# A two-layer diffusion trunk on one core: the tile scheduler ranks instructions by a simulated timeline

## The chip, the core and the metric

The kernel runs on one core of a Trainium2 chip. The core has five engines, each with a queue of its own that it works through in order: TensorE (PE in the profile; its weight loads are shown apart, as PEld), VectorE (DVE), ScalarE (ACT), GpSimd (POOL) and SyncE (SP, which here only issues DMA transfers). An instruction that needs another engine's result waits for a semaphore, and all that stands behind it in its queue waits with it. So the order in each queue is a part of the program, although it changes nothing in what is computed.

The metric is the device time of one execution in microseconds; below 1% matters here. The median of three runs of the kernel before is 1856.94 us.

## What is computed

Two layers over 512 latent tokens and 256 context tokens, width 1024. The first mixes by neighbourhood attention and spatial gating, the second by retention in both directions; each layer ends in a gated MLP with a convolution over three tokens. Everything is float32.

```python
for i in range(DEPTH):
    ...
    h_lat = modulate(rmsnorm(x, norm_g[i, 0]), sh1, sc1)
    h_ctx = modulate(rmsnorm(xc, norm_g[i, 0]), csh1, csc1)
    if i % 2 == 0:
        y_ctx, y_lat = hybrid_na_sgu(...)
    else:
        y_ctx, y_lat = retention_mixer(...)
    x = x + g1 * rmsnorm(y_lat, norm_g[i, 1])
    h = modulate(rmsnorm(x, norm_g[i, 2]), sh2, sc2)
    x = x + g2 * rmsnorm(conv_ffn(h, ...), norm_g[i, 3])
    ...

def conv_ffn(h, w_in, conv_w, conv_b, w_out):
    a = dwconv3(h @ w_in, conv_w, conv_b)
    gate, up = jnp.split(a, 2, axis=-1)
    return (jax.nn.silu(gate) * up) @ w_out
```

## The kernel before

Every float32 operand of a matmul is split into a high part, rounded by ACT, and a low part, the rest, subtracted by DVE (`split`, line 110); three matmuls (`mm3`, line 152) make a product of them: high by high, high by low, low by high. So each weight that a DMA brings in costs one ACT and one DVE instruction of about 1 us before PE can use it, and in the names of the profile `g` or `fo` stand for both parts. Most instructions are issued by one wrapper and so carry its line, L71; the names of the tiles tell them apart.

The stages, with their place in the profiled span:

- Start and spatial gating (0 to about 150 us): `sgu` (line 725) loads the tokens, makes the modulation rows `ad` from the ada weights (`ar`), and turns and scales the tokens (`xT`, `first_xT` line 1778) into the operands `h0a`/`h1a` (`first_h`, line 1788). The first products are `ug`, with weights `ug10` to `ug13` in four steps `q`; in the program each step makes its weights' split, then the three token chunks of h0a, then the products, with ada rows between.
- Attention (to about 400 us): head pairs; `take_qk` (line 946) makes the operands of the scores. `kb`, the low part of k beside itself, is made by DVE in pieces and then doubled by POOL (line 970). `pq`, `s`: projections and scores. The gate rows of later stages are made beside it (`acc <- ar` on DVE, 256 instructions in the whole kernel).
- First MLP, `ffn(0)` (line 1439; to about 930 us): 768 tokens, 22 blocks `j` of 128 hidden columns. Per block the two halves, gate and up, come from seven block products instead of eight: the accumulators `px`, `py`, `pz` take products with the weights `wa`, `wb` (from `s`), `wc` (from `q`) and `wd`; ACT and DVE move them to `pre` (`take`, `meet`), and `conv` (line 1531) makes `cv`, then `g`. The weights of block j+1 are prepared between the products of block j. The output product `wf` with weights `fo` is made per pair of blocks in 12 pieces that are strewn between products of later blocks; ACT copies each piece (`yp`, `ypg`) and POOL issues a DMA that adds it in memory. The last four blocks, 18 to 21, are left to `out_last` (line 635), which adds blocks 18 and 19 (group A, tiles `wf0A`) for the first tokens and then blocks 20 and 21 (group B) into the same accumulators.
- Retention (to about 1450 us): operands `h0c`/`h1c` from `build_h` (line 417), weights `rwv`, `rwg`, `wx` and others, products `rn`.
- Second MLP, `ffn(1)` (to the end): the same with 512 tokens; its last output groups (`wf1A`, `wf1C`) end the kernel.

What sets the order. The program is written as one sequence. [...] Which tiles share a buffer follows from the program, and so do all dependencies. Some stretches are exempt: between `hold(True)` and `hold(False)` (line 367) every instruction of DVE, ACT and PE is marked to keep its place in program order against other marked ones (`Ordered`, line 59). These marks stand around the closing output pieces (`out_pieces`, line 599, only where `final` is given), the norms behind them (`flush`, line 709) and the first products of an MLP. The products and convolutions of the blocks and the group A pieces of `out_last` are not marked:

```python
LAST = NF - 2 * GF
...
    product(X, d[22], hb(("t", 4)), "onto")
    take(pre, 1, 0, X)
    step()
    o(3)
    gs[j] = conv(j, pre)
...
self.out_group(*A, y, e, False, None, f"{name}A", "CB", held=held)
...
self.out_group(*B, y, e, False, final, f"{name}B", held=held)
```

## Time and profile before

| | before |
|---|---|
| median of 3 runs | 1856.94 us (1853.55 to 1860.03) |
| profiled execution | 1852.3 us, of this span 1850.5 us |
| PE, PEld, DVE, ACT, POOL busy | 96%, 86%, 75%, 56%, 18% |
| mean granted PE clock | 0.99 |
| DMA | 253.45 MB, mean 137 GB/s |

How to read it: a row of the timeline gives the start and the length of an instruction or of a run of equal ones, the engine, the line, the operation, out <- in by the program's names, the shape and the count; in brackets, how long the engine had been idle before it and what ended that. Rows of equal matmuls are drawn together, also where some stand among others. A row of the windows gives the busy time of each engine in a stretch, with the count, then the clock that PE was granted (1.00 is full speed), the busy share of the DMA engines and what they moved. The list of waits sums an engine's idle time by the operand that ended it.

### The profile page before, as it was taken

How to read it: one execution, taken by the hardware profiler on the slowest of the kernel's cores; microseconds unless marked ns; L12 is line 12 of the kernel's file. 1: busy time of each engine (PE TensorE's matmuls, PEld its weight loads, DVE VectorE, ACT ScalarE, POOL GpSimd, SP SyncE). 2: the span in 40 equal slices, each digit the busy share in tenths (PEclk: the TensorE clock that was granted, in tenths of full speed). 3: DMA queues.
4: the chain of work that ended last, by engine and by line, in shares of the span. 5: the costliest groups of instructions: out<-in, count | busy, mean ns of one | idle time of the engine just before them, and what ended most of it. 6: DMA issues, size and time to landing. Idle time of an engine off the chain costs nothing. (4 is left out here: it accounts for less than half of the span.)

```text
span 1850.5 us, 28777 instructions
## 1 busy us (share of the span) xinstructions
PE 1781.8 (96%) x10928; PEld 1582.7 (86%) x10928; DVE 1391.1 (75%) x2347; ACT 1029.3 (56%) x1866; POOL 330.0 (18%) x462
## 2 busy tenths in 40 slices
PE   7999899999999999999999999999999889999997
PEld 4888777679998899998888988988999789989996
DVE  4877675789878788787866676676656699988886
ACT  6533455677555565564664534344434467766763
POOL 1102122131122322222112011011101100222221
PEclk9999999999999999999999999999999989999999
DMA  7344321155577777786722422331321225877762
GB/s 297 112 141 143 117 82 36 55 171 148 178 156 168 174 175 161 156 173 151 265 97 92 143 99 80 125 113 58 105 69 60 101 82 157 215 197 201 171 161 97
DMA packets 84399, 253.45 MB, mean 137 GB/s; under 512 B 11026, under 2 KB 11538, under 8 KB 84260
## 3 DMA queue, kind: packets, MB, share of 16 engines
q1 hardware_dynamic: 55044, 191.27, 30.9%
q0 software_dynamic: 26912, 51.95, 16.4%
q10 hardware_dynamic: 2304, 8.39, 1.1%
q8 instruction: 86, 1.41, 0.3%
q14 instruction: 53, 0.43, 0.1%
HBM read 191.80 MB, written 39.85 MB: 125 GB/s over the span
## 5 line engine op out<-in xcount | busy, mean ns | idle before, releaser
L71 DVE SCALAR_TENSOR_TENSOR acc<-ar,cs,acc 128x512 f32<-128x512 f32 x256 | 185.7, 751 | 33.7 <-DMA ar<-in_adaw 24.7
L71 DVE SCALAR_TENSOR_TENSOR cv<-pre,cw,cv 128x769 f32<-128x769 f32 (+1 forms) x176 | 153.6, 884 | 4.9 <-ACT cv L71 4.2
L71 PE MATMUL rn<-rwv,h0c 128*128 128x256 f32 x768 | 136.3, 281 | 3.0 <-ACT h0c L71 3.0
L71 PEld LDWEIGHTS rn<-rwv,h0c 128*128 128x128 f32 x768 | 118.2, 191 | 3.7 <-ACT h0c L71 3.4
L71 PE MATMUL wf<-fo,g 128*128 128x512 f32 x432 | 112.6, 394 | 0.5 <-DVE fo L71 0.5
L71 PE MATMUL rn<-rwv,h1c 128*128 128x256 f32 x384 | 108.1, 282 | 0.4 <-DVE h1c L71 0.2
L1688 POOL DMA_DIRECT2D yf<-yp x64 | 55.1, 861 | 257.0 <-ACT yp L71 233.8
L71 ACT ACTIVATE cv<-pre,cw 128x770 f32<-128x770 f32 (+1 forms) x88 | 81.3, 925 | 24.0 <-DVE pre L71 23.4
L71 PE MATMUL rn<-rwg,h0c 128*128 128x256 f32 x512 | 90.0, 280 | 0.0
L71 PEld LDWEIGHTS wf<-fo,g 128*128 128x128 f32 x432 | 75.9, 188 | 13.8 <-DVE fo L71 1.4
L71 PE MATMUL px<-hs,wc 128*128 128x384 f32 (+1 forms) x480 | 79.3, 314 | 5.4 <-ACT pre L71 3.2
L71 PEld LDWEIGHTS px<-hs,wc 128*128 128x128 f32 x480 | 74.3, 191 | 10.8 <-ACT pre L71 5.4
L71 ACT ACTIVATE pre<-px 128x256 f32<-128x256 f32 (+2 forms) x160 | 54.3, 367 | 47.7 <-PE px L71 47.6
L71 ACT COPY yp<-wf 128x512 f32<-128x512 f32 x118 | 67.8, 576 | 19.0 <-PE wf L71 16.5
L71 PEld LDWEIGHTS rn<-rwg,h0c 128*128 128x128 f32 x512 | 78.1, 189 | 0.0
L71 PE MATMUL pz<-hb,wa 128*128 128x384 f32 (+1 forms) x480 | 77.3, 308 | 0.0
L71 PE MATMUL px<-hb,wa 128*128 128x384 f32 (+1 forms) x480 | 77.1, 308 | 0.0
L71 PE MATMUL py<-blk,wb 128*128 128x384 f32 (+1 forms) x480 | 76.9, 308 | 0.0
L71 PE MATMUL px<-blk,wb 128*128 128x384 f32 (+1 forms) x480 | 76.7, 309 | 0.0
L71 PEld LDWEIGHTS px<-hb,wa 128*128 128x128 f32 x480 | 73.2, 188 | 3.2
L71 PEld LDWEIGHTS px<-blk,wb 128*128 128x128 f32 x480 | 73.4, 189 | 3.0 <-ACT pre L71 0.2
L71 PEld LDWEIGHTS rn<-rwv,h1c 128*128 128x128 f32 x384 | 72.9, 190 | 1.5 <-DVE h1c L71 1.3
(1272 smaller groups left out, 5112.6 us busy)
## 6 DMA issues: line engine op xcount, KB each, us to landing
ar<-in_adaw SPq DMA_DIRECT2D x96, 512.0 KB, 3.9
yf<-yp POOLq DMA_DIRECT2D x64, 256.0 KB, 4.2
yd<-yp POOLq DMA_DIRECT2D x54, 256.0 KB, 5.0
yd<-ypg POOLq DMA_DIRECT2D x54, 256.0 KB, 4.9
fin<-xd SPq DMA_DIRECT2D x8, 512.0 KB
xn<-in_x SPq DMA_DIRECT2D x6, 512.0 KB, 4.6
xb<-in_x SPq DMA_DIRECT2D x6, 512.0 KB
xd<-xb ACTq DMA_DIRECT2D x6, 512.0 KB, 2.8
```

Source lines behind the costliest of these rows:

```text
L71: i = f(*args, **kw)
L1688: G.dma_start((yd[t] if first else y[t])[:, o], v, accum_op=ALU.add)
```

## The change

One argument at the place where the framework is opened:

```diff
-    with tile.TileContext(nc) as tc, ExitStack() as ctx:
+    with tile.TileContext(nc, schedule_with_timeline_sim=True) as tc, ExitStack() as ctx:
         Trunk(ctx, tc, a, out).build()
```

[...] The order within each engine's queue changes, and with it which instruction carries a wait.

## The prediction

> **What bounds the kernel now.** I read the summary of the page first, then the chain of waits, the waits of PE, and the windows; times within the span count from its start.
>
> ```profile
> span 1850.5 us, 28777 instructions
> ...
> PE 1781.8 (96%) x10928; PEld 1582.7 (86%) x10928; DVE 1391.1 (75%) x2347; ACT 1029.3 (56%) x1866; POOL 330.0 (18%) x462
> ...
> PE 35%; DVE 7%; DMA 3%; ACT 2%; issue 1%; POOL 1%; ACTq 0%; DVEq 0%; POOLq 0%
> ```
>
> TensorE is busy for 1781.8 of 1850.5 us, and both kernels issue the same matmuls. So an order can gain at most what PE stands idle, 1850.5 - 1781.8 = 68.7 us, and it can lose without such a limit. The waits of PE say where these idle times lie (columns: total, times, longest).
>
> ```profile
> PE ht L71 <- DVE xn L71: 9.4, 1, 9.4
> PE s L71 <- POOL kb L970: 7.1, 1, 7.1
> PE pf L71 <- ACT hb L71: 5.9, 1, 5.9
> PE px L71 <- ACT pre L71: 3.2, 4, 1.2
> ...
> PE at L71 <- ACT arow L71: 2.4, 1, 2.4
> PE px L71 <- ACT wc L71: 2.2, 1, 2.2
> PE wf L71 <- ACT ypg L71: 2.1, 2, 1.6
> ...
> PE wf L71 <- DVE fo09l L71: 1.8, 1, 1.8
> ```
>
> No wait is large. The first (9.4, the first load) and `pf <- hb` (5.9, the norm between retention and the second MLP) stand at places whose order the two kernels share; they stay. The windows add the engines behind PE and the clock:
>
> ```profile
> core 0: us, PE busy (x) PEld busy (x) DVE busy (x) ACT busy (x) POOL busy (x), PEclk, DMA share, GB/s
> 435.00:445.00 10.00, 9.18 (x51) 8.43 (x50) 10.00 (x13) 10.00 (x16) 0.00 (x0) 1.00 0.17 52
> ...
> 500.00:850.00 350.00, 346.60 (x1802) 320.62 (x1801) 281.23 (x401) 201.52 (x348) 92.08 (x117) 1.00 0.76 167
> ...
> 1550.00:1851.00 301.00, 288.81 (x1972) 265.12 (x1971) 256.10 (x398) 192.58 (x346) 62.73 (x76) 0.99 0.67 172
> ...
> 190.00:197.00 7.00, 4.93 (x13) 4.06 (x14) 6.03 (x10) 5.43 (x11) 3.88 (x2) 0.51 0.47 149
> 640.00:644.00 4.00, 4.00 (x13) 3.37 (x13) 4.00 (x8) 2.69 (x4) 1.17 (x2) 0.58 0.75 180
> 862.00:870.00 8.00, 8.00 (x44) 7.49 (x43) 6.18 (x11) 3.61 (x7) 2.61 (x3) 1.00 0.84 228
> ```
>
> Inside the MLPs PE is full (346.6 of 350), with DVE behind it at 80% (281.23) and 85% (256.10); at the head of the first MLP DVE and ACT have no free time at all. The last three rows are for the clock, below.
>
> **The change, part by part.** It adds and removes no instruction: comparing the two programs, every name and operation has its partner. 6195 of 10832 matmuls, 1448 of 2251 DVE, 1012 of 1730 ACT, 71 of 462 POOL and 86 of 400 SP instructions stand in another place of their queue. A matmul that is moved among others costs nothing by itself, since the matmuls run back to back (40 in 9.31 us, below); what costs is an operand that is now late for its place. So I laid the new order over the times of the profiled run and looked for places where an instruction would come before its operand. Nearly all that I found are at stage borders.
>
> Second MLP, last product (+4.4):
>
> ```profile
> 1817.47 1.65 PE L71 MATMUL px<-hs 128*128 128x256 f32 x12
> 1818.95 9.31 PE L71 MATMUL wf1A<-fo,g 128*128 128x512 f32 x40
> ...
> 1819.15 0.38 ACT L71 ACTIVATE pre<-px 128x256 f32<-128x256 f32 x1 [0.23 <-PE px L71]
> ...
> 1822.79 0.63 ACT L71 ACTIVATE g<-cv 128x512 fp32r<-128x512 f32 x1 [1.63 <-DVE cv L71]
> ...
> 1823.46 0.69 DVE L71 TENSOR_TENSOR g<-cv,g 128x512 fp32r<-128x512 f32 x1 [0.70 <-ACT g L71]
> ```
>
> The last product px ends at 1819.1; evacuation, convolution and gate take until the high part g is there (1822.79 + 0.63 = 1823.4) and its low part (1824.15). Now 24 output matmuls of earlier blocks, 24 x 9.31 / 40 = 5.6 us, lie over this chain. The new order puts 21 of the 24 ahead of the last product and leaves 3. The work is the same, but the chain starts 21 x 0.233 = 4.9 us later and PE has 0.7 us to do instead of 5.6: by the times, PE would stand 4.4 us ahead of the high part, 4.7 of the low. I take 4.4; if the chain ran faster with DVE and ACT less loaded, 3.5.
>
> First MLP, last product (+6.5), the same mechanism with longer tiles:
>
> ```profile
> 894.38 2.25 PE L71 MATMUL px<-hs,wd 128*128 128x384 f32 x12
> ...
> 897.40 0.40 PE L71 MATMUL wf0A<-fo018h,g 128*128 128x512 f32 x1
> ...
> 903.54 0.40 PE L71 MATMUL wf0A<-fo020h,g 128*128 128x512 f32 x1
> ...
> 901.97 0.85 ACT L71 ACTIVATE g<-cv 128x770 fp32r<-128x770 f32 x1 [2.21 <-DVE cv L71]
> ...
> 902.85 0.96 DVE L71 TENSOR_TENSOR g<-cv,g 128x770 fp32r<-128x770 f32 x1 [0.92 <-ACT g L71]
> ```
>
> From px's end (896.6) to g's high part (902.8) is 6.2 us, to its low part (903.8) 7.2. The output matmuls and gate rows from 896.5 to 903.5 cover it; the new order moves them up to 21 us forward and again leaves 3 (0.7 us). 5.5 to 6.5 stay uncovered; laid over the times it is 7.0 to 7.5. I take 6.5, bounds 4 (the chain on emptier ACT and DVE queues) and 7.5.
>
> Start (+3.5):
>
> ```profile
> 25.96 0.57 ACT L71 COPY xT<-ht 128x512 f32<-128x512 f32 x1
> 26.43 0.64 ACT L71 ACTIVATE h0a<-xT 128x512 fp32r<-128x512 f32 x1
> ...
> 28.98 1.05 ACT L71 ACTIVATE ug<-ug11r 128x1024 fp32r<-128x1024 f32 x1
> ...
> 27.49 0.73 PE L71 MATMUL ug<-ug,h0a 128*128 128x512 f32 x2
> ```
>
> ACT now makes the first h0a at 26.43 and then splits ug11. The new order has the splits of ug11 and ug12 (1.05 each) and two to three more copies of 0.57 ahead of h0a: 2 x 1.05 + 2.5 x 0.57 = 3.5. PE's queue has its first two ug matmuls ahead of the ada products that could run meanwhile, so they queue behind the wait. On SP two 0.5 MB loads for these splits go out before the ada rows. Bounds 0 (the ada rows come later anyway) and 4.4.
>
> Head of the first MLP (+3):
>
> ```profile
> 443.12 2.38 PE L71 MATMUL px<-hs,wc 128*128 128x384 f32 x12 [0.43 <-ACT pre L71]
> ...
> 458.38 1.07 ACT L71 ACTIVATE fo02h<-fo02r 128x1024 fp32r<-128x1024 f32 x1
> ```
>
> fo02h, for a block two steps on, is split at 458.4; in the new order it and wa of block 4 stand in ACT's queue ahead of the convolution of block 1 and of the reads of block 2's px (DVE's likewise). Where its load or its bank comes late, all that stands behind it waits, and so does PE's next product for block 2: 3 to 6.3 us by the order, of which 2.5 is what the same overlay gives for the old order. Bounds 0 and 6.
>
> Entry into retention (+1.5), the last pair of attention heads (+1.5) and the retention heads (+1):
>
> ```profile
> 949.53 1.06 ACT L71 ACTIVATE wx<-rwq0r 128x1024 fp32r<-128x1024 f32 x1
> 950.48 1.05 ACT L71 ACTIVATE rwg<-rwg00r 128x1024 fp32r<-128x1024 f32 x1
> ...
> 949.18 0.80 PE L71 MATMUL rn<-rwv,h0c 128*128 128x256 f32 x2 [2.14 <-ACT h0c L71]
> ```
>
> PE waits 2.14 here already. Two weight splits more stand ahead of the third h0c, some 2 us, partly covered by the first rn products: 0 to 4.5. The other two are short slips of 1 to 2.4 us in the overlay.
>
> **Clock.** After 7.1 us without matmuls the clock is 0.51 for 7 us (190 to 197); after the 1.8 us for fo09l it is 0.58 for 4 us; after the 2.4 us for arow it stays 1.00. A half-rate stretch of 3.4 us costs 1.7, one of 6.8 costs 3.4. For the two MLP tails I add 1.7 each, +3.4; bounds 0 and 8.5 (five stalls).
> [...]
>
> Gains (-7.7). `s <- kb`: the new order has one score matmul and ten pq matmuls (0.23 each) ahead of it, but kb's last DVE piece goes behind more splits (1.2): 7.1 becomes 4.8, -2.3 (-4 to +1). `at <- arow` is filled with a px product: -2.4. For fo09l, ypg and wc (1.8, 2.1, 2.2), matmuls of the next block are put ahead: -3 of 6.1 (-6 to 0).
>
> The sum: 4.4 + 6.5 + 3.5 + 3 + 1.5 + 1.5 + 1 + 3.4 - 7.7 = +17.1 us. The profiled execution took 1852.3 (1850.5 in the span); the median of three is 1856.94, 4.6 more. 1856.9 + 17.1 = 1874.
>
> **Rivals.**
> *Faster: the tails cost nothing and the gaps close.* Place: the two last products. If PE reaches its earlier work sooner, the last px isn't later than now, and what the overlay calls a stall is time won before. Then the gains stand alone: kb 4, arow 2.4, fo09l, ypg, wc 6.1 at most, px on pre 3.2, and a half-rate stretch at 640 with 1.7: 17 at the most; 10 as a middle gives 1847. For it: these waits are real idle time. Against it: PE is full ahead of both tails, so that 21 matmuls ahead of the product delay it by just their time.
> *No change.* The borders cost half of what I have (10 of 21) and the gains come in full (10): about 1857. For it: DVE and ACT at a border do the same work in any order.
> *Much slower.* Inside the MLPs DVE is at 80 to 85%. If look-ahead splits delay convolution and evacuation in every block as at the head, some 36 inner blocks of both MLPs lose 1 us each: +36 on top, 1910. For it: DVE's and ACT's queues are reordered everywhere. Against: the overlay shows slips of under 1 us there.
> That the change does nothing is excluded, as over half of the matmuls move.
>
> **How the numbers follow.** Forecast 0.60, faster 0.13, no change 0.13, much slower 0.14. A measurement of this kernel tells about 0.3% (5.6 us) from no change: 1851.4 to 1862.5. Faster: 0.11 of the first rival and 0.01 of the second, 0.12. Same: 0.02 + 0.11 = 0.13. Slower: 0.75. The forecast's own range, from the bounds: losses (24.8 in all) at half with the gains as taken, 12.4 - 7.7 = +4.7, to losses at one and a half with gains of 2, 37.2 - 2 = +35.2: 1862 to 1892. To hold 8 in 10 it reaches into no change and part of much slower: 1852 to 1900.
>
> **What would show it.** Right: in the waits of PE new rows `wf1A <- g` of about 4 us and `wf0A <- g` of about 6, each with a half-rate window behind; the first `ug` matmuls some 3 us later; `s <- kb` below 5 and `at <- arow` gone; PE's busy time up by the half-rate matmuls only. Wrong: no wait on g at either tail (the faster rival), or the 500 to 850 and 1550 to 1800 stretches longer by over 10 us with many short waits on pre (the much slower one).

## The result, and the profile after

The changed kernel takes 1887.26 us (median of 4 runs, 1884.94 to 1888.16), the kernel before, run beside it, 1856.61 (4 runs, 1853.55 to 1860.03). The ratio is 1.0163, with a 95% interval of 1.0143 to 1.0183: the new order costs 30.65 us. The forecast of 1874 had the sign and half of the size. The profiled execution of the changed kernel took 1886.85 us, 34.5 more than that of before, so the traces carry about 4 us more than the medians.

The head of the page of the changed kernel, with its chain of waits:

```profile
span 1885.0 us, 28860 instructions
...
PE 1792.7 (95%) x10928; PEld 1592.8 (84%) x10928; DVE 1389.6 (74%) x2347; ACT 1023.8 (54%) x1866; POOL 332.9 (18%) x462
...
PE 37%; DVE 6%; DMA 3%; ACT 2%; issue 1%; POOL 0%; DVEq 0%; POOLq 0%; ACTq 0%
```

The same 10928 matmuls, and PE is busy 10.9 us longer (1792.7 - 1781.8): that is matmuls at a lower clock (mean granted clock 0.981, before 0.990; in the stretches at a clock of 0.50 PE is busy for 49.65 us, before for 25.32), as the windows below show in part. (So the busy time of PE is no floor, as the prediction's limit of 68.7 us took it to be: an order changes it too.) The other 23.6 us of the longer span are idle time of PE. DVE and ACT have no more work than before. The list of PE's waits of the changed kernel (total, times, longest) says where:

```profile
PE ht L71 <- DVE xn L71: 8.2, 1, 8.2
PE wf0A L71 <- ACT g L71: 6.3, 1, 6.3
PE pq L71 <- ACT vt L71: 5.9, 1, 5.9
PE pf L71 <- ACT hb L71: 5.6, 1, 5.6
PE rn L71 <- ACT h0c L71: 4.3, 3, 2.1
PE wf1A L71 <- ACT g L71: 4.3, 1, 4.3
...
PE wf L71 <- ACT fo00h L71: 3.5, 1, 3.5
PE ht L71 <- ACT xT L71: 2.5, 2, 1.8
PE ug L71 <- ACT h0a L71: 2.5, 2, 1.9
PE wf L71 <- ACT g L71: 2.4, 2, 1.5
PE px L71 <- ACT pre L71: 2.3, 1, 2.3
PE adt L71 <- ACT mr L71: 2.3, 2, 1.3
PE py L71 <- ACT pre L71: 2.0, 1, 2.0
```

Gone are `s <- kb` (7.1 before), `at <- arow` (2.4), `rt <- rg` (2.8), `px <- wc` and `wf <- ypg`. New are `wf0A <- g`, `wf1A <- g` and `pq <- vt`, and a number of short waits at the start, at the head of the first MLP and at the entry into retention. Behind them the windows of the changed kernel (busy time of the engines with counts, then PE's clock) show the clock drop:

```profile
core 0: us, PE busy (x) PEld busy (x) DVE busy (x) ACT busy (x) POOL busy (x), PEclk, DMA share, GB/s
20.00:30.00 10.00, 7.45 (x36) 4.57 (x35) 7.69 (x14) 9.83 (x18) 0.49 (x1) 0.78 0.98 372
30.00:40.00 10.00, 10.00 (x41) 5.58 (x39) 3.77 (x5) 2.71 (x4) 0.00 (x0) 0.87 0.61 213
70.00:80.00 10.00, 10.00 (x39) 8.12 (x38) 8.72 (x21) 4.41 (x8) 0.00 (x0) 0.83 0.26 81
...
458.00:462.00 4.00, 4.00 (x12) 3.62 (x13) 4.00 (x5) 1.61 (x2) 0.00 (x0) 0.50 0.82 260
500.00:850.00 350.00, 347.42 (x1802) 319.29 (x1801) 283.40 (x407) 202.42 (x356) 89.31 (x114) 1.00 0.75 170
925.00:930.00 5.00, 4.47 (x10) 3.31 (x11) 1.74 (x3) 1.20 (x3) 0.00 (x0) 0.50 1.02 419
...
970.00:980.00 10.00, 4.85 (x19) 3.54 (x17) 7.41 (x10) 8.58 (x13) 1.55 (x2) 0.56 0.62 175
...
1855.00:1865.00 10.00, 7.71 (x24) 6.12 (x25) 5.91 (x10) 2.73 (x7) 1.36 (x2) 0.66 0.00 2
```

The row from 500 to 850 is nearly the same as before (347.42 of 350 here, 346.6 there): the inner blocks of the first MLP lose nothing.

A list of waits can't tell a wait that is new from one that only pays back time won earlier. So I compared the two kernels at equal work: from all matmul rows of both traces, the time at which PE has begun as many matmul columns as the kernel before at a given place of its span. The difference is how far the changed kernel is behind there. I use this "lag at equal work" for all runs below; it is my own computation, not a view of the profile. As the rows draw equal matmuls together, a value is good to about 1 us.

```
place (us in the span of before)     lag of the changed kernel, us
start                  30 / 74       4.3 / 9.7
attention             374 / 438      10.0 / 11.0
head of first MLP     444 / 450 / 510   15.2 / 19.8 / 20.1
its inner blocks      855            20.2
its tail              900 / 905 / 910   15.7 / 21.9 / 23.7
entry into retention  950 / 960      23.6 / 28.6
retention            1160 / 1490     26.2 / 24.2
second MLP, inner    1560 / 1810     28.2 / 27.9
its tail             1831            34.7
```

The loss falls in short stretches at stage borders, as forecast, but not in the sizes that were forecast.

### The profile page after: what moved, and what is told of

It reads as the page before. It is cut to its first block, busy times and chain, and to the rows that moved or that the text cites. A ratio compares the mean times of both kernels' runs of the same rounds, so it can differ in the third digit from the quotient of the medians.

```text
span 1885.0 us, 28860 instructions
## 1 busy us (share of the span) xinstructions
PE 1792.7 (95%) x10928; PEld 1592.8 (84%) x10928; DVE 1389.6 (74%) x2347; ACT 1023.8 (54%) x1866; POOL 332.9 (18%) x462
## 5 line engine op out<-in xcount | busy, mean ns | idle before, releaser
L71 DVE SCALAR_TENSOR_TENSOR cv<-pre,cw,cv 128x769 f32<-128x769 f32 (+1 forms) x176 | 154.6, 883 | 20.5 <-ACT cv L71 19.5
L71 PE MATMUL rn<-rwv,h0c 128*128 128x256 f32 x768 | 141.9, 284 | 4.5 <-ACT h0c L71 4.3
L71 PE MATMUL px<-hb,wa 128*128 128x384 f32 (+1 forms) x480 | 88.1, 313 | 2.3 <-ACT wa L71 1.1
L71 PEld LDWEIGHTS wf<-fo,g 128*128 128x128 f32 x432 | 76.4, 189 | 15.7 <-ACT g L71 2.7
L71 PEld LDWEIGHTS px<-hb,wa 128*128 128x128 f32 x480 | 77.0, 190 | 9.5 <-ACT wa L71 2.6
L71 PE MATMUL pz<-hb,wa 128*128 128x384 f32 (+1 forms) x480 | 84.2, 309 | 0.0
L71 PE MATMUL py<-blk,wb 128*128 128x384 f32 (+1 forms) x480 | 81.9, 309 | 2.3 <-DVE wb L71 1.1
L71 PEld LDWEIGHTS py<-blk,wb 128*128 128x128 f32 x480 | 73.6, 188 | 5.1 <-ACT wb L71 1.7
L71 PEld LDWEIGHTS pz<-hb,wa 128*128 128x128 f32 x480 | 74.3, 189 | 2.3
```

The costliest lines, as they stand in the source:

```text
L71: i = f(*args, **kw)
```

## The experiments

Two kinds. The first four start from the changed kernel and put one stretch back by marks that keep an instruction behind the one that was issued just ahead of it in the program on its engine (not, as the section on the kernel before has it, behind other marked ones). The other eight start from the kernel before: a chain of order edges fixes, for each engine, the old order everywhere except in one stretch of the program, where the instructions stand in the new order. The runs compare the two orders; how the scheduler comes to either is shown by none of them. All compute the same as before. The marks leave the scheduler free to order the rest anew: e1_tail and e4_ret differ from the changed kernel only near their stretch, but e2_start also in the places of 359 matmuls between 472 and 613 us, and e3_head in PE's order up to 760 us. The kernel before had a median of 1858.14 (7 runs) beside the first four, and of 1858.09, 1859.08 and 1857.35 (16 to 20 runs) beside the others. The changed kernel ran only beside the 1856.61 above, so a difference to its median carries some 1.5 us of that.

### Tails of the MLPs put back (e1_tail)

```diff
+                self.tail = T.hold = j == NF - 1
                 product(X, d[22], hb(("t", 4)), "onto")
...
-            self.T.hold = bool(final) and t not in free
+            self.T.hold = bool(final) and t not in free or self.tail
```

> The changed kernel, with marks on PE that keep the last block product px of each MLP ahead of the output matmuls of group A (wf0A, wf1A), as they stand in the program. Theory (the cover was moved ahead of the chain that it covered): the waits wf0A <- g (6.3 us) and wf1A <- g (4.3 us) fall below 1 us each, the half-rate stretches behind them go, and the time falls by 11 to 14 us, to about 1874. Rival (the output matmuls that were moved forward fill gaps ahead of the product, which open again when they are moved back; the changed kernel gained 4.5 us between 855 and 895 us): the waits go, but PE waits that much more ahead of the product, and the time falls by 5 us or less, to 1882 or more.

Measured: 1881.59 (4 runs), ratio to before 1.0129 [1.0098, 1.0160], so 5.7 us off the changed kernel's median: between the two forecasts, nearer to the rival's. Both waits on g are gone; PE's longest waits between 850 and 930 us of this kernel are:

```profile
PE px L71 <- ACT pre L71: 2.3, 2, 1.7
PE at L71 <- ACT arow L71: 1.2, 1, 1.2
```

At the first tail the lag now goes from 23.4 (855) to 22.9 (910), -0.5 instead of +3.5; at the second from 28.4 to 30.3, +1.9 instead of +6.6. So 4.0 and 4.7 come back, not the 6.3 + 4.3 of the waits with their half-rate stretches (in the changed kernel PE is busy for 4.70 us at 0.50 from 923.40 to 930.23 us and for 4.78 from 1855.24 to 1862.07). At the first tail the reason is in the table above: the new order is 4.5 us ahead (20.2 to 15.7) when it reaches the wait, because the moved output matmuls have filled earlier gaps. Program order gives up this lead together with the wait. The rest of the 8.7 is lost again elsewhere (+1.6 from 785 to 810 us, where PE waits 1.4 us for wa).

### The first loads in program order (e2_start)

```diff
-        self.nc.sync.dma_start(out, src)
+        i = self.nc.sync.dma_start(out, src)
+        if self.Q:
+            self.tc.keep_in_program_order(i)
```

`Q` is true from the first ada rows to the end of the first operands.

> The changed kernel, with marks on SP alone that keep the loads of the start (ada rows ar, weights ug) in program order, so that the ug loads come behind the ada rows. Theory (the start loses 10 us by equal work because ug loads stand ahead of ada rows in SP's queue, and adt, h0a and the second and third step wait for these): the loss at 75 us falls from 10 to 3 us or less, and the time by 5 to 8 us, to about 1880. Rival (the order on ACT and PE is the cause, as the prediction put it: splits ahead of h0a, two ug matmuls ahead of the ada products): the loss at 30 us stays above 3 and that at 75 us above 7, the time is 1884 or more.

Measured: 1901.12 (4 runs), ratio 1.0230 [1.0203, 1.0257]: 14 us worse than the changed kernel. Its first half came out as the theory has it: at 30 and 42 us the lag is 0.7 and 0.2 instead of 4.3 and 3.8. But then it is 7.7 at 62 and 16.6 at 74. In strict program order the loads of ug12 and ug13 stand on SP behind ada rows that wait for a free buffer; a row of the timeline of this kernel shows who pays:

```profile
43.22 1.06 ACT L71 ACTIVATE ug<-ug12r 128x1024 fp32r<-128x1024 f32 x1 [3.02 <-DMA ug12r<-in_hyb_ug]
```

ACT waits 3.02 us for that load with the next copies behind it. The first 4 us can't be put down to SP's order alone: with the later loads, ACT's splits of ug11 and ug12 stand behind the first h0a again (at 28.14 and 43.22 us here, 22.41 and 24.84 in the changed kernel), and PE's wait for xT falls from 2.5 to 1.0 us. So theory and rival, the loads and the splits, are not told apart by this run. Neither the new nor the program's order of the loads is the right one there.

### Block sums in program order (e3_head)

```diff
                 sums = self.block_sums(l)
+                S.hold = V.hold = first
...
                 steps[3]()
+                S.hold = V.hold = False
```

> The changed kernel, with marks on DVE and ACT that keep the head of the first MLP (block sums, the convolutions of blocks 0 and 1 and the weights of block 2) in program order. Theory (DVE has the weight sums of block 2, which wait for a load, ahead of the last pieces of the block sums; the sums' two rounds of DMA come late, and ACT stands at hs with the reads of pf, fo00h and wa behind it): ACT's wait for sb <- sa (3.1 us) and PE's for fo00h (3.5) go, the loss between 438 and 456 us falls from 9 to 3 us or less, the time by 5 to 9 us, to about 1880. Rival (DVE and ACT are full there, so whatever is put first, something else is late): the loss stays above 6 and moves to another operand, time 1884 or more.

Measured: 1891.43 (4 runs), ratio 1.0181 [1.0147, 1.0216], no better than the changed kernel. ACT no longer waits for the sums, but the lag from 438 to 450 us grows by 16.0 (8.6 to 24.6) instead of 8.8, and PE's waits from 445 to 475 us of this kernel are:

```profile
PE wf L71 <- ACT fo00h L71: 3.1, 1, 3.1
PE wf L71 <- ACT fo01h L71: 2.5, 1, 2.5
PE wf L71 <- DVE fo00l L71: 1.9, 1, 1.9
PE py L71 <- ACT wb L71: 1.7, 1, 1.7
```

With the sums held, the splits for the output weights become late: the wait moves to another operand, as the rival has it, though neither engine is full in this run (of the 30 us from 440, DVE is busy for 25.6 and ACT for 20.1). The late sums alone are not shown as the cause by this run; w_headA below takes the place by itself.

### Entry into retention put back (e4_ret)

```diff
                     k_ctx(h, wk)
-                    self.hold(False)
+                    T.hold = False
...
                     decay(h)
+                    S.hold = V.hold = False
```

> The changed kernel, with marks on DVE and ACT that keep the splits of wx, rwg00, rwg01 and the two decay tables behind the splits of h0c at the entry into retention. Theory (these splits ahead of h0c cost what the prediction says): of the 5 us lost by equal work between 945 and 960 us all goes, and PE's waits for h0c and h1c fall from 6.0 to 3 us or less; the time falls by 3 to 6 us, to about 1882. Rival (the splits are only late somewhere else: wx and rwg are then late for rq and the gate products): the time does not fall, 1886 to 1888, with waits of PE on wx or rwg.

Measured: 1882.64 (4 runs), ratio 1.0122 [1.0092, 1.0152]. From 945 to 960 us the lag goes from 25.4 to 25.0; in the changed kernel it grows by 5.0 (23.6 to 28.6). PE's waits from 940 to 1000 us of this kernel:

```profile
PE rn L71 <- ACT h0c L71: 3.1, 2, 2.3
PE rn L71 <- DVE h1c L71: 0.8, 3, 0.4
```

That is what the kernel before has (3.0 on h0c). The medians of the two kernels differ by 4.6 us, the growth of the lag at the entry by 5.4. Only 9 instructions of ACT and 5 of DVE stand elsewhere than in the changed kernel. So the splits (with the two decay tables) put ahead of the last h0c are the cause, at over three times their forecast of 1.5.

### One stretch in the new order (w_start, w_head, w_t0, w_t1)

The same edit makes all eight kernels of this kind; ORDER holds for each engine the list of instruction numbers, and only the stretch differs.

```diff
+    for names in ORDER:
+        for ahead, i in zip(names, names[1:]):
+            tc.add_manual_dep(traced[i], ahead, edge, reason="in_order")
...
         Trunk(ctx, tc, a, out).build()
+        in_order(tc, nc)
```

The stretches: w_start, everything up to the last ada row of the first modulation; w_head, instructions 3990 to 5000, from the last input pieces of the first MLP to its block 4; w_t0, blocks 20 and 21 of the first MLP with the closing groups; w_t1, the last block of the second MLP with its closing groups.

> All engines held to the old order, except that the instructions of the start (the first gating products, up to the last ada row of the first modulation) stand in the new sequence, in the same places. Theory (the loss of about 10 us by equal work at 75 us belongs to the order of this stretch alone): 9 to 11 us by 80 us, and the time 8 to 11 us above the kernel before, 1866 to 1868. Rival (it came from outside, such as from the loads and gate work of the next stage, which the new order moves in between): below 5 us.

> The old order, except for the head of the first MLP (last pieces of its input, block sums, blocks 0 to 4), which stands in the new sequence. Theory (block sums late on DVE, hs late on ACT, as the changed kernel shows): a loss of 8 to 10 us between 430 and 460 us with ACT waiting for sb <- sa, time 1865 to 1868. Rival (the loss needs the later arrival that the changed kernel had from the attention's end): 4 us or less.

> The old order, except for blocks 20 and 21 of the first MLP and its closing output groups, which stand in the new sequence. Cover theory of the prediction: the wait wf0A <- g of 6 us and a half-rate stretch behind it cost 8 us, less the filled wait at <- arow (2.4): time 1862 or more. Rival (from the run with the marks, where taking the wait away brought only a third of it: the pieces moved forward fill gaps ahead of the last product): the wait is there, but the net is +2 to +4, time 1859 to 1861.

> The old order, except for the last block of the second MLP and its closing output groups, which stand in the new sequence. Cover theory: wait wf1A <- g of 4.3 us, half-rate stretch 1.7 us, time 5 to 6.5 us above the kernel before (1862 to 1864). Rival (the pieces moved forward fill gaps): +1 to +3 us.

| | median (runs) | ratio [interval] | lag inside the stretch |
|---|---|---|---|
| w_start | 1867.68 (4) | 1.0053 [1.0033, 1.0073] | +7.9 at 74 us |
| w_head | 1873.53 (4) | 1.0082 [1.0064, 1.0099] | -1.1 (410) to +10.9 (492) |
| w_t0 | 1859.57 (10) | 1.0012 [0.9998, 1.0027] | +1.5 (855), -3.1 (900), +5.1 (910) |
| w_t1 | 1865.97 (7) | 1.0031 [1.0015, 1.0048] | +9.4 (1810) to +15.5 (1828) |

The start alone reproduces 7.9 of the 9.7 us, and the head alone is the dearest stretch. In w_t0 the wait is there in full, and the kernel is hardly slower:

```profile
PE wf0A L71 <- ACT g L71: 6.3, 1, 6.3
```

4.6 us are won before it (1.5 to -3.1), 8.2 are lost at it, 3.6 remain. In w_t1 there is no such lead, and the lag grows by 6.1 us: the 4.3 of the wait, and about what the half-rate stretch behind it cost in the changed kernel (half of the 4.78 us at 0.50, an estimate of 2.4). In w_head the lag grows by another 3.3 at 585 us. This, and the lags of 9.4 at 1810 in w_t1 and of 1.5 at 855 in w_t0 lie outside the changed stretches; the last section is about these.

### The stretches that should gain, together (w_gain)

New order in the attention (instructions 1632 to 3400), in blocks 20 and 21 of the first MLP without the output groups, and in retention from 9420 to 14300.

> The old order, except for three stretches in the new sequence, in which the changed kernel gained by equal work: the first four of five parts of the attention (75 to 340 us: 6 us gained), blocks 20 and 21 of the first MLP without the output groups behind them, so that the cover stays (855 to 900 us: 4.5), and the retention heads behind the entry (1000 to 1400 us: 3). Theory (the gains belong to the order of these stretches and add up): no wait of 7 us for kb, none for arow, 8 to 13 us below the kernel before, 1845 to 1850. Rival (they were only the taking back of delays from ahead of them, as work that is late finds its operands ready): 3 us or less, 1855 or more.

Measured: 1866.22 (9 runs), ratio 1.0038 [1.0024, 1.0051]: slower. The theory falls; the rival's bound (1855 or more) holds, but its reason does not give a loss. The lag shows leads that are paid back. Attention: 0.8 to -2.8 (290 us), then +5.3 (338). First MLP: 5.7 to 0.8 (895), then +11.7 (910). Retention: 12.2 (1000) to 8.3 (1330), then 12.1 (1440). The waits of PE where two of these were paid back, in this kernel:

```profile
PE pq L71 <- ACT vt L71: 6.1, 1, 6.1
...
PE s L71 <- DVE sc L71: 3.7, 2, 2.8
...
PE px L71 <- DVE pre L71: 5.9, 1, 5.9
```

In the attention the wait on kb did not get shorter but moved to vt, and at the tail the wait on g moved to pre. In retention the stretch ended in the middle of a head, and the waits (`rn <- gt` 1.5, `kn <- m1k` 1.1) stand where the two orders meet.

### The head in two halves (w_headA, w_headB)

w_headA: instructions 3990 to 4380 (last input pieces, block sums, block 0, products of block 1). w_headB: 4381 to 5000 (convolution of block 1, blocks 2 to 4).

> The old order, except for the first part of the head of the first MLP (last pieces of its input, block sums, block 0 and the products of block 1), which stands in the new sequence. Theory (the loss that the prediction did not have: weight sums of block 2 and splits ahead of the block sums on DVE, sums 7 us late, ACT behind hs): most of the loss is here, 7 us or more between 430 and 460 us. Rival (the prediction's: splits of fo02 and block 4 ahead of the convolution of block 1): 3 us or less here.

> The old order, except for the second part of the head of the first MLP (convolution of block 1, blocks 2 to 4 with their weights and fo00 to fo04), in the new sequence. Theory of late block sums: 4 us or less between 430 and 500 us. Rival, the prediction's mechanism (splits of fo02 and block 4 ahead of the convolution of block 1 and the reads of px): 3 to 6 us, and nearly nothing in the other part.

Measured: w_headA 1867.80 (4 runs), ratio 1.0041 [1.0025, 1.0056]; w_headB 1864.29 (10 runs), 1.0034 [1.0020, 1.0049]. Together they make about the 12.0 of w_head: the lag grows from 0.6 (438) to 8.2 (450) in w_headA, and from 1.2 to 4.4 (6.2 at 492) in w_headB. PE's longest wait there, first in w_headA:

```profile
PE wf L71 <- ACT fo00h L71: 6.2, 1, 6.2
```

and in w_headB:

```profile
PE px L71 <- ACT pre L71: 2.9, 1, 2.9
```

The second is the mechanism of the prediction (splits ahead of convolution and evacuation), at 3.2 to 5.0 where it has 3. ACT stands 3.27 us at the load of fo02 in w_headB, and 4.12 us in the changed kernel, with the end of block 1's convolution and the reads of block 2's px behind it:

```profile
463.73 1.06 ACT L71 ACTIVATE fo02h<-fo02r 128x1024 fp32r<-128x1024 f32 x1 [4.12 <-DMA fo02r<-in_ffn_out]
```

The first, at 8 the larger, is one that the prediction does not have. Four rows of the changed kernel's timeline show it:

```profile
425.56 0.69 DVE L71 TENSOR_TENSOR s<-f012r 128x512 f32<-128x512 f32 x1 [1.60 <-DMA f012r<-in_ffn_in]
...
434.46 1.82 DVE L71 TENSOR_TENSOR sb<-sb,sb 128x768 f32<-128x768 f32 x2
...
449.82 3.05 ACT L71 ACTIVATE hs<-sb 128x768 fp32r<-128x768 f32 x4 [3.06 <-DMA sb<-sa]
454.82 1.06 ACT L71 ACTIVATE fo00h<-fo00r 128x1024 fp32r<-128x1024 f32 x1
```

DVE takes weight work for block 2 ahead of the block sums `sb` and waits 1.60 us for its load. The sums come at 434.5. In the timeline of the kernel before the first of them stands 15 us earlier, of which 11 is lag that the changed kernel has there already:

```profile
419.42 0.95 DVE L71 TENSOR_TENSOR sb<-sb,sb 128x768 f32<-128x768 f32 x1
```

The sums go through memory (`sa`) and back, and ACT, which is to round them to `hs`, stands 3.06 us at the head of its queue until 449.8. Behind hs stand the evacuations, the gate of block 0 and the split fo00h, and PE's first output matmuls wait for the latter. In w_headA, which has no lag before this place, the sums begin 4.1 us later than in the kernel before (423.55 us), hs 3.7 later (437.05 against 433.38), and ACT's g of block 0, now behind all four hs, 6.7 later (440.80 against 434.14). So the late sums make about half of the delay and ACT's own order the rest; no run takes these two apart.

### Retention alone (w_ret2)

New order in instructions 9420 to 14640: the retention heads to the end of their stage.

> The old order, except for the retention behind its entry, up to the last output group and with it, in the new sequence: a stretch that ends at a border, so that nothing is cut off that could be paid back there. Theory (a lead by equal work inside a stage is work moved forward, which is paid back where the stage ends; the kernels compared by equal work show -4.4 us inside this stage): within 1 us of the kernel before at 1475 us, time 1857 to 1861. Rival (the retention has a gain of its own of 3.5 us, from 28.6 at its entry to 24.9 at its end in the changed kernel): -3 us or more at 1475 us, time 1853 to 1856.

Measured: 1850.53 (12 runs, 1847.55 to 1856.35) against 1857.35 (17 runs, 1853.55 to 1862.84): ratio 0.9967 [0.9954, 0.9980]. This is faster than both kernels. The rival is right. The lag is -0.1 at 950, -2.9 at 1160 and -4.7 at 1490. The window from 1000 to 1100 us shows much of the gain, in this kernel:

```profile
1000.00:1100.00 100.00, 99.61 (x650) 90.97 (x651) 68.49 (x118) 46.69 (x70) 13.26 (x18) 0.98 0.41 127
```

and in the kernel before:

```profile
1000.00:1100.00 100.00, 96.14 (x615) 85.17 (x615) 68.47 (x121) 47.04 (x69) 16.44 (x18) 1.00 0.33 110
```

PE is busy for 99.61 us instead of 96.14, at a slightly lower clock (the counts of 650 and 615 are of matmuls of mixed sizes). The two waits `rt <- rg` (2.8) and those on ah (1.3) are gone: PE has products of the next step (`rq`) ahead of the last of them. So the theory that every lead is paid back does not hold in retention.

## Why the prediction was right, and where it was wrong

The sign was right, and so was the kind: the inner blocks kept their pace and the stage borders lost. The terms, each as the growth of the lag over its place:

| term | forecast | measured |
|---|---|---|
| start | +3.5 | +9.7 |
| attention (kb, last pair) | -0.8 | +1.3 |
| head of the first MLP | +3 | +9.1 |
| gains at fo09l, ypg (first MLP) and wc (head of the second MLP) | -3 | +0.1 and +3.9 |
| tail of the first MLP with clock and arow | +5.8 | +3.5 |
| entry into retention | +1.5 | +5.0 |
| retention heads | +1 | -4.4 |
| tail of the second MLP with clock | +6.1 | +6.6 |
| sum | +17.1 | +34.7 |

The single sizes are worse than the sum shows. Start, head, entry and the places of the gains came out 22.8 us dearer than forecast, the retention heads and the first tail 7.7 cheaper. That the time lies within the range is in part owed to its width.

Point by point:

**Tail of the second MLP.** Right in mechanism, and the size came out. The changed kernel's timeline has the row that was named as its sign:

```profile
1851.47 1.54 PE L71 MATMUL px<-hs 128*128 128x256 f32 x12
...
1856.61 0.63 ACT L71 ACTIVATE g<-cv 128x512 fp32r<-128x512 f32 x1 [2.33 <-DVE cv L71]
...
1857.29 4.99 PE L71 MATMUL wf1A<-fo,g 128*128 128x512 f32 x11 [4.28 <-ACT g L71]
```

4.28 us of waiting where 4.4 was forecast, and a half-rate stretch behind it (0.66 from 1855 to 1865 us). w_t1 and e1_tail bear it out from both sides (6.1 and 4.7). That the wait came so near is in part luck. By the rows that the prediction shows, the chain of 4.3 us (1819.1 to 1823.4) less 0.7 of cover leaves 3.6 ahead of the high part; 4.4 is the stall ahead of the low part. And the 0.7 of cover was not there: px ends at 1853.0, and PE begins nothing until 1857.29.

**Tail of the first MLP.** The wait (6.3) and its half-rate stretch (0.50 from 925 to 930 us) came as forecast, but the net loss is 3.5. The step that failed is that the moved matmuls were costed as a pure delay of the last product: "PE is full ahead of both tails, so that 21 matmuls ahead of the product delay it by just their time". PE was not full ahead of this one, and filling its gaps won 4.5 us (4.6 in w_t0). Of these, 2.4 are the wait `at <- arow`, which the prediction had booked as a gain; the 2 us that it had not are three short waits of the kernel before in blocks 20 and 21, `px <- pre` (1.0 and 0.4) and `wf <- ypg` (0.4). The "faster" rival had this part right.

**Start.** The step that failed is the late first h0a. The splits of ug11 and ug12 stand ahead of it as forecast, but it begins at 26.75 us (26.43 before), and the sign named for it did not come: the first ug matmul begins at 27.44 us, against 27.49 before.

```profile
26.42 1.12 PE L71 MATMUL ht<-ident,xn 128*128 128x128 f32 x4 [1.75 <-ACT xT L71]
27.44 2.07 PE L71 MATMUL ug<-ug,h0a 128*128 128x512 f32 x4
```

What the splits hold up are copies xT ahead of h0a, for which PE's transposes wait (`ht <- xT` 2.5). PE then runs at half rate, and the prediction gave the start no half-rate matmuls; the windows at 20 to 40 and 70 to 80 us have 0.78, 0.87 and 0.83, which is about 5 us at full rate. The waits `ug <- h0a` (2.5) and `adt <- mr` (2.3) come behind 40 us, at later pieces. The step "On SP two 0.5 MB loads for these splits go out before the ada rows" was named and given no price. Whether it has one of its own is open: e2_start moves the splits together with the loads.

**Head of the first MLP.** The forecast's 3 is what w_headB measures (3.2 to 5.0). The missing 8 lies where w_headA has it: at the block sums' round through memory behind a DVE queue that waits for a load, and at hs ahead of the gate on ACT. The place is shown by the run; the cause is read from the rows, and holding the sums alone (e3_head) did not win it back. The overlay moved instructions against the times of PE, DVE and ACT, but kept the loads' and the sums' arrival as they were.

**Entry into retention.** The mechanism was right (e4_ret takes the 5.0 away), the size wrong: "some 2 us, partly covered by the first rn products" left out that PE would stall in several places and then run at 0.56 (970 to 980 us; the kernel before has 0.77 from 945 to 960).

**Gains.** `s <- kb` did not go to 4.8: it disappeared, and PE waits nearly as long (5.9 against 7.1) one step earlier, for vt. Two rows of the changed kernel's timeline:

```profile
194.82 0.75 DVE L71 SCALAR_TENSOR_TENSOR acc<-ar,cs,acc 128x512 f32<-128x512 f32 x1 [3.19 <-DMA acc<-in_adab_row]
198.88 0.79 PE L71 MATMUL pq<-h0a,wq 128*128 128x512 f32 x1 [5.89 <-ACT vt L71]
```

DVE stands 3.19 us at a load for a later stage's gate rows just ahead of it, with kb's pieces behind; whether this load decides the wait for vt was not tried. At fo09l PE still waits 1.5 us. The waits for ypg and wc are gone, but what that won was paid back: the lag falls from 20.5 (570 us) to 18.8 (575) and is 19.9 at 620; at the head of the second MLP it falls from 26.8 (1515) to 22.8 (1520) and is 28.4 at 1540. There other waits come right behind (among them `py <- pre` 2.0 and one of 1.5 for `wf <- g`). The prediction has no term for this head but the gain at wc; its 3.9 us were not tried by themselves, so their cause stays open.

**Retention heads.** Forecast as a small loss, in truth the one real gain: -4.4 in the changed kernel, -4.5 in w_ret2. The overlay looked for operands that come too late and did not look for PE time before `rt <- rg` that could be filled.

**The rivals.** "Much slower" fell: the inner blocks lost 0.1 us, not 1 each. "No change" fell: the gains in the whole kernel are one stage's. "Faster" fell at both tails: at the second PE had no gap to fill, and at the first 3.5 us stayed lost.

## What to carry to other kernels

When a scheduler moves filler work forward, compare at equal work and not wait by wait: a lead that fills a gap is worth something only if the serial chain at the end of the stage still has cover, and look there first. The dear case here was an instruction that waits for a load, put early in its queue by the new order, with the stage's own serial work behind it (1.60 us of waiting on DVE for f012r, 4.12 on ACT for fo02r): so cost the queue behind the wait, DMA queues and half-rate matmuls too. A new order need not be taken whole: here all of it costs 1.6%, and its retention stage alone gains 0.3%.

## What was not expected of the hardware

The same order ran differently from one execution to the next, here by a half-rate window. In w_ret2 everything from 580 to 660 us stands in the order of before. PE waits for fo09l in both, 1.8 us before, and in w_ret2

```profile
PE wf L71 <- DVE fo09l L71: 2.2, 1, 2.2
```

The window behind it, in w_ret2

```profile
640.00:660.00 20.00, 20.00 (x107) 18.64 (x106) 18.53 (x29) 11.33 (x20) 5.14 (x6) 1.00 0.82 174
```

and in the kernel before

```profile
640.00:660.00 20.00, 20.00 (x97) 18.32 (x97) 17.66 (x26) 11.31 (x19) 4.28 (x5) 0.91 0.77 173
```

The longer wait is followed by the full clock and 107 matmuls, the shorter one by 0.91 and 97: in the kernel before PE runs at 0.50 from 640.63 to 644.05 us. What decides between the two is not shown by these runs.

Something like it is in retention: `rt <- rg` waits 1.6 us at the longest in the profile of before, but 2.7 in w_t0 and w_t1, which have the same order there:

```profile
PE rt L71 <- DVE rg L71: 5.2, 3, 2.7
```

(w_t1, 976 to 1475 us: 5.2 in three waits, where before has 2.8 in two.) So one profile of an order is good to some 3 us in a stretch, and over the whole kernel to more: w_start drifts from 7.1 behind at 910 us to 13.2 at the end, in the order of before. This is why the lags above are read inside the changed stretch only, and why w_t1 is 9.4 behind before its stretch begins.
